# The last head pair's sample retention among its query projections, its norm in two parts, and attention's loads in memory of their own

## The chip, the cores and the metric

The kernel runs on one core of one Trainium2 chip. The metric is the device time of one execution in microseconds, as the median of several timed runs. A core has five engines that run their own instruction streams side by side and wait for each other by semaphores: TensorE (PE in the profile, its weight loads PEld), VectorE (DVE), ScalarE (ACT), GpSimd (POOL) and SyncE (SP, which issues most of the DMAs).

## The reference

One decoder layer over a prompt of 1024 tokens and 8 x 4 sample tokens. A combined projection of width 3912 feeds two groups of heads: sparse attention (8 heads, the top 256 keys chosen by an indexer) and retention (8 heads of 64, in chunks of 128 with a state carried from chunk to chunk). Each group's output is gated, both go through one output projection, a norm and a gated embedding. What the change touches is the retention, its head norm and gate, and the beginning of attention:

```python
def _head_norm(o):
    mu = jnp.mean(o, axis=-1, keepdims=True)
    var = jnp.mean(jnp.square(o - mu), axis=-1, keepdims=True)
    return (o - mu) * lax.rsqrt(var + EPS)
...
    def step(S, inp):
        qc, kc, vc = inp
        inter = jnp.einsum('bchk,bhkv->bchv', qc * dec_in[None, :, :, None], S)
        scores = jnp.einsum('bchk,bshk->bhcs', qc, kc) * dmat[None]
        intra = jnp.einsum('bhcs,bshv->bchv', scores, vc)
        S = S * dec_chunk[None, :, None, None] + jnp.einsum('bchk,bchv->bhkv', kc * dec_out[None, :, :, None], vc)
        return S, inter + intra
...
    logits = jnp.einsum('bqngd,bqknd->bqngk', qg, kg.astype(jnp.float32)) * (HEAD_DIM ** -0.5)
...
    logits = jnp.where(sel_ok[:, :, None, None, :], logits + bias, -jnp.inf)
    probs = jax.nn.softmax(logits, axis=-1)
    o = jnp.einsum('bqngk,bqknd->bqngd', probs, vg.astype(jnp.float32))
...
    yb = jax.nn.silu(gb) * _head_norm(ob).reshape(B, T, D_B).astype(x.dtype)
```

The retention runs once over the prompt (8 chunks of 128 tokens, state 0 at the start) and once over the samples (one chunk of 4 tokens for each of 8 requests, with a state that is read from memory and written back).

## The kernel before

The work goes in phases: the input norm and the indexer's scores, the sample's selection of keys, the retention, attention over the prompt with the sample's attention woven in, the output projection, and the gated embedding. A scheduler of the framework orders each engine's instructions; between them the order is by the sequence of the code, by priority, and by what is ready in its own reckoning. Semaphores are placed after that. An engine never passes over a waiting instruction.

The retention loops over four pairs of heads (hp 0 to 3). For a pair it makes, in this order: the sample's q and k (mm_s, 32 rows, L274, summed from four partial results by a copy on ACT, L276, and three adds on VectorE, L279); for each of eight blocks of 128 tokens (tb) a q/k projection into a PSUM bank named pqk (mm_a, 24 matmuls, L265 to L267), rotated by rope (three VectorE products L1034 to L1036 into tiles rp, one buffer each, then two additions on POOL, L1038 and L1039); then the rotation of the sample's q and k; the sample's v and gate (mm_s again); and for each block a v/g projection (bank pvg). ACT takes v and the gate out of that bank (L1047, L1049). Then the chunk's recurrence follows: transposes (L1055, L1056), a copy of qkT by ACT (L1060), scores (L1065), the decay mask by VectorE (sm, L1066), the state update (L1456, sbd L1461), two products (L1465, L1467) and a copy of the result into acc (L1469). pqk and pvg take turns in the same three PSUM banks.

At block 7 comes the sample's retention, ret_sample: its state s0 is loaded, qm (VectorE, L1113) and eight products L1116 (16 matmuls in the profile) apply it, L1118 adds the scores' part, L1120 and L1122 collect it in acc, vm (L1127) and dst (L1129) make the new state, sso (L1133, L1134), which is stored (L1135). qm, vm and sso share one memory (tag vm). Last comes norm_gate, over the eight prompt blocks and then over the sample's rows: statistics (L1075, L1076), a root on ACT with one refinement on VectorE (L1081 to L1090), the scaling on ACT and VectorE (L1094, L1096), the gate (L1099, for the last pair on VectorE) and the store into yb_d (L1100). acc has one buffer, so the next pair's results wait for that store.

steps(hp) weaves in the sample's selection (bits oh, L1246, matmuls psl, L1248, then le, row and idx, L1252 to L1260, which feed POOL's gathers L1147).

Attention goes over eight query blocks (qb) and two key heads (kv). For each it makes near (L1550, the position bias from toep), scores sa on TensorE (L1563, L1564, a bank of three), their masked sum and row minimum mn on VectorE (L1569), the exponential on ACT (L1572), transposes ptp and a copy pT, the product ob with the values vtok, and the reciprocal sums spread by rb. Its loads are qas (queries, two buffers), toep, vtok and the keys ka. The first weights of the output projection (o0) are loaded, cast (L179) and subtracted (L180) by load_w.

The sample's retention and the norm in the last pair stand here:

```python
            if tb == 7:
                sgS = ret_sample(hp, qks[8], sh, acc)
        steps(hp)
        ...
        norm_gate(acc, sgs, 8, 128, 0, hp)
        norm_gate(acc[:, 8:9, :], [sgS], 1, NS, 8, hp)
```

## Time and profile before

| what | value |
|---|---|
| median of 3 runs | 1076.51 us (1073.67 to 1078.84) |
| profiled execution | 1065.73 us, its span 1063.9 us |
| granted TensorE clock, mean | 0.973 |
| busy, share of the span | PE 93%, PEld 79%, DVE 66%, ACT 47%, POOL 27% |
| last v/g projection of the last pair | starts at 636.19 us |
| first attention scores | start at 651.86 us |

The profiled execution is one run with the profiler on; its time is 1% below the median of the timed ones. Times in its rows count from the start of the span. A row of the timeline has the start, the duration, the engine, the line, the operation, output and inputs by the program's names, partitions x elements and type, a count, and in brackets the idle time ahead of it with what ended it. A row of a window has its length and the busy time of each engine with the number of instructions, then the granted TensorE clock (1 is full), the DMA engines' mean share and GB/s.

### The profile page before, as it was taken

How to read it: one execution, taken by the hardware profiler on the slowest of the kernel's cores; microseconds unless marked ns; L12 is line 12 of the kernel's file. 1: busy time of each engine (PE TensorE's matmuls, PEld its weight loads, DVE VectorE, ACT ScalarE, POOL GpSimd, SP SyncE). 2: the span in 40 equal slices, each digit the busy share in tenths (PEclk: the TensorE clock that was granted, in tenths of full speed). 3: DMA queues.
4: the chain of work that ended last, by engine and by line, in shares of the span. 5: the costliest groups of instructions: out<-in, count | busy, mean ns of one | idle time of the engine just before them, and what ended most of it. 6: DMA issues, size and time to landing. Idle time of an engine off the chain costs nothing.

```text
span 1063.9 us, 19686 instructions
## 1 busy us (share of the span) xinstructions
PE 991.7 (93%) x7375; PEld 838.6 (79%) x7375; DVE 699.8 (66%) x2012; ACT 504.2 (47%) x1092; POOL 288.1 (27%) x287
## 2 busy tenths in 40 slices
...
GB/s 291 65 60 51 79 96 169 186 145 202 126 164 111 70 40 41 37 48 87 61 24 41 119 86 149 190 79 105 75 56 47 117 41 80 148 111 82 86 37 40
DMA packets 98308, 102.24 MB, mean 96 GB/s; under 512 B 21346, under 2 KB 88386, under 8 KB 95906
## 3 DMA queue, kind: packets, MB, share of 16 engines
...
## 4 chain that ended last, share of the span: by engine, by line
PE 53%; DVE 8%; ACT 2%; DMA 2%; issue 1%; POOL 1%; SPq 0%; DVEq 0%; ACTq 0%; POOLq 0%
PE ob L1587 4%; PE ptp L1579 4%; PE pg L265 3%; PE pg L267 3%; PE pg L266 3%; PE po L265 3%; PE po L266 2%; PE po L267 2%; PE pvg L265 2%; PE pvg L266 2%; PE pvg L267 2%; PE sa L1563 2%; PE sa L1564 2%; PE pqk L265 2%; PE pqk L266 1%; PE pqk L267 1%
## 5 line engine op out<-in xcount | busy, mean ns | idle before, releaser
L1147 POOL DMA_INDIRECT kvs<-in_cache_kv,idx x64 | 63.6, 994 | 84.1 <-ACT pT L1584 44.7
L265 PE MATMUL pqk<-whi_qkb,xh 128*128 128x256 f32 x256 | 74.5, 291 | 5.5 <-DVE rp L1036 5.5
L265 PE MATMUL pvg<-whi_vgb,xh 128*128 128x256 f32 x256 | 77.4, 302 | 1.6 <-DVE need L729 1.5
L266 PE MATMUL pvg<-wlo_vgb,xh 128*128 128x256 f32 x256 | 76.6, 299 | 0.0
L267 PE MATMUL pvg<-whi_vgb,xl 128*128 128x256 f32 x256 | 75.2, 294 | 0.0
L266 PE MATMUL pqk<-wlo_qkb,xh 128*128 128x256 f32 x256 | 73.5, 287 | 0.0
L265 PE MATMUL po<-whi_o,yTh 128*128 128x256 f32 x256 | 73.1, 286 | 0.4 <-DVE yaT L1598 0.4
L267 PE MATMUL pqk<-whi_qkb,xl 128*128 128x256 f32 x256 | 73.0, 285 | 0.0
L267 PE MATMUL po<-whi_o,yTl 128*128 128x256 f32 x256 | 72.8, 285 | 0.0
L265 PE MATMUL pg<-whi_g,yTh 128*128 128x256 f32 x256 | 72.7, 284 | 0.0
L266 PE MATMUL po<-wlo_o,yTh 128*128 128x256 f32 x256 | 72.7, 284 | 0.0
L267 PE MATMUL pg<-whi_g,yTl 128*128 128x256 f32 x256 | 72.3, 282 | 0.0
L266 PE MATMUL pg<-wlo_g,yTh 128*128 128x256 f32 x256 | 72.2, 282 | 0.0
L500 DVE SCALAR_TENSOR_TENSOR score<-r,wi,score 128x384 f32<-128x384 f32 (+5 forms) x42 | 44.2, 1053 | 21.0 <-ACT r L496 19.9
L1572 ACT ACTIVATE L<-L,mn 128x128 f32<-128x128 f32 (+7 forms) x64 | 49.5, 775 | 13.7 <-DVE mn L1569 13.6
L265 PEld LDWEIGHTS pqk<-whi_qkb,xh 128*128 128x128 f32 x256 | 48.2, 188 | 9.6 <-issue 6.8
L1768 DVE TENSOR_TENSOR sgm<-pu,sgm 128x256 f32<-128x256 f32 x32 | 13.5, 423 | 61.8 <-PE pu L267 58.6
L265 PEld LDWEIGHTS pvg<-whi_vgb,xh 128*128 128x128 f32 x256 | 50.6, 197 | 3.7 <-issue 1.7
L266 PEld LDWEIGHTS pvg<-wlo_vgb,xh 128*128 128x128 f32 x256 | 50.7, 198 | 0.5
L267 PEld LDWEIGHTS pvg<-whi_vgb,xl 128*128 128x128 f32 x256 | 50.6, 198 | 0.6
L265 PEld LDWEIGHTS po<-whi_o,yTh 128*128 128x128 f32 x256 | 49.0, 191 | 2.2 <-issue 1.6
L496 ACT ACTIVATE r<-si 128x384 f32<-128x384 f32 (+5 forms) x48 | 36.3, 758 | 30.3 <-PE si L354 29.0
...
## 6 DMA issues: line engine op xcount, KB each, us to landing
...
```

Source lines behind the costliest of these rows:

```text
L265: nc.tensor.matmul(pt[:, :n], ah, hi[:, k, :n], start=(k == 0), stop=False)
L266: nc.tensor.matmul(pt[:, :n], ah, lo[:, k, :n], start=False, stop=False)
L267: nc.tensor.matmul(pt[:, :n], al, hi[:, k, :n], start=False, stop=(k == kc - 1))
L496: nc.scalar.activation(r[:, :n], s[:, :n], AF.Relu)
L500: nc.vector.scalar_tensor_tensor(sc, r[:, :n], wi[:, qb, h:h + 1], sc, op0=ALU.mult, op1=ALU.add)
L1147: return nc.gpsimd.indirect_dma_start(out=dst, out_offset=None, in_=kvflat, in_offset=bass.IndirectOffsetOnAxis(ap=idx, axis=0))
L1563: nc.tensor.matmul(s[:, :wc], qas[:, h, :], kah[kv][:, c:c + wc], start=True, stop=False)
L1564: nc.tensor.matmul(s[:, :wc], qas[:, h, :], kal[kv][:, c:c + wc], start=False, stop=True)
L1572: behind[0] = nc.scalar.activation(L[:, :n], L[:, :n], AF.Exp, bias=least, scale=-1.0, accum_out=sm[:, i4:i4 + 1])
L1579: nc.tensor.transpose(tp[:, i4 * 128:i4 * 128 + 128], P[i4][:, kb * 128:kb * 128 + 128], ident)
L1587: nc.tensor.matmul(ob[64 * o:64 * o + 64, :256], vtok[:, kb, kv * 64:kv * 64 + 64], pT[:, o * 256:o * 256 + 256], start=(kb == 0), stop=(k ...
L1768: nc.vector.tensor_tensor(sg[:rows], usrc, sg[:rows], op=ALU.mult)
```

## The change

For the last pair (hp 3) the sample's q and k are rotated ahead of block 0; at block 4 of the q/k projections the sample's v and gate are projected and its retention is made; at block 4 of the v/g projections the sample's rows and blocks 0 to 3 are normed and gated; blocks 4 to 7 are normed at the end. The other pairs keep their order. Attention's queries, toep and vtok get a pool of their own on the other side of the memory, opened ahead of the keys' loads. One bank of the scores' phase is set aside first (lfirst), which turns the order in which the others are handed out. The first output weights' load is put behind the exponentials of the third query block.

```diff
--- before.py
+++ after.py
@@ -1433,16 +1433,22 @@
         sh = mm_s(bank("pqk"), xs, wqk, 256, rt, f"qk{hp}")
         wvg = load_w(f"vgb{hp}", wcols((VB + hp * 128, 128), (GB + hp * 128, 128)))
         qks = []
+        if hp == 3:
+            qk8 = rope(sh, NS, 8, f"{hp}_8")
         for tb in range(8):
+            if hp == 3 and tb == 4:
+                acc = rt.tile([128, 9, 128], F32, tag="acc", bufs=1, name=f"acc{hp}")
+                sh = mm_s(bank("pvg"), xs, wvg, 256, rt, f"vg{hp}")
+                sgS = ret_sample(hp, qk8, sh, acc)
             pt = bank("pqk")
             mm_a(pt, xlhs, wqk, 256, tb)
             qks.append(rope(pt, 128, tb, f"{hp}_{tb}"))
             steps(hp)
-        qks.append(rope(sh, NS, 8, f"{hp}_8"))
-        acc = rt.tile([128, 9, 128], F32, tag="acc", bufs=1, name=f"acc{hp}")
         sgs = []
-        sh = mm_s(bank("pvg"), xs, wvg, 256, rt, f"vg{hp}")
         if hp < 3:
+            qks.append(rope(sh, NS, 8, f"{hp}_8"))
+            acc = rt.tile([128, 9, 128], F32, tag="acc", bufs=1, name=f"acc{hp}")
+            sh = mm_s(bank("pvg"), xs, wvg, 256, rt, f"vg{hp}")
             wnext = load_w(f"qkb{hp + 1}", wcols((QB + (hp + 1) * 128, 128), (KB + (hp + 1) * 128, 128)))
         for tb in range(8):
             pt = bank("pvg")
@@ -1467,16 +1473,22 @@
                 nc.tensor.matmul(o[:, j * 64:j * 64 + 64], sm[:, j, :], vv[:, j * 64:j * 64 + 64],
                                  start=(tb == 0 and j == 0), stop=(j == 1))
             nc.scalar.copy(acc[:, tb, :], o)
-            if tb == 7:
+            if tb == 7 and hp < 3:
                 sgS = ret_sample(hp, qks[8], sh, acc)
+            if hp == 3 and tb == 4:
+                norm_gate(acc[:, 8:9, :], [sgS], 1, NS, 8, hp)
+                norm_gate(acc, sgs, 4, 128, 0, hp)
         steps(hp)
         so = rt.tile([128, 64], F32, tag="so", bufs=2, name=f"so{hp}")
         for j in range(2):
             js = slice(j * 64, j * 64 + 64)
             nc.vector.tensor_scalar(so[js], sbd[0][js, js], gend[js, hp:hp + 1], None, op0=ALU.mult)
         nc.sync.dma_start(O["ret_state_prompt"][0, 0, 2 * hp:2 * hp + 2].rearrange("h d v -> (h d) v"), so)
-        norm_gate(acc, sgs, 8, 128, 0, hp)
-        norm_gate(acc[:, 8:9, :], [sgS], 1, NS, 8, hp)
+        if hp < 3:
+            norm_gate(acc, sgs, 8, 128, 0, hp)
+            norm_gate(acc[:, 8:9, :], [sgS], 1, NS, 8, hp)
+        else:
+            norm_gate(acc[:, 4:8, :], sgs[4:], 4, 128, 4, hp)
     rt_stack.close()
     bss_.close()
 
@@ -1484,6 +1496,22 @@
         for _ in ss:
             pass
     ka = [wp.tile([128, 2, T], F32R, tag=f"w{t}", bufs=2, name=f"ka{t}") for t in ("hi", "lo")]
+    pres = ExitStack()
+    pre = pres.enter_context(pool("pre"))
+    vtok = pre.tile([128, 8, 128], F32, name="vtok")
+    toep = pre.tile([128, 8, 256], F32, name="toep")
+
+    def load_q(qb):
+        q = pre.tile([128, 8, 128], F32R, tag="qas", bufs=2, name=f"qas{qb}")
+        last_q[0] = nc.sync.dma_start(q.bitcast(F32), qas_d[:, :, qb * 128:(qb + 1) * 128]).ins
+        return q
+
+    last_q = [None]
+
+    qnext = load_q(0)
+    nc.sync.dma_start(toep, bass.AP(tensor=toep_d.tensor, offset=toep_d.offset + 127,
+                                    ap=[[8 * 384 - 1, 128], [384, 8], [1, 256]]))
+    nc.sync.dma_start(vtok, v_d)
     kah, kal = ([t[:, i] for i in range(2)] for t in ka)
     for i in range(2):
         for a, t in enumerate((kah[i], kal[i])):
@@ -1499,25 +1527,12 @@
     yaT = yap.tile([128, 4, T], F32, name="yaT")
     psum_phase(b=3, t=2, l=1, o=1)
     kept["tags"] = "s"
+    bank("lfirst", "l")
     as_ = ExitStack()
     ap_ = as_.enter_context(pool("att", side="right"))
     a1 = ExitStack()
     atl = a1.enter_context(pool("atl", side="right"))
     at = a1.enter_context(pool("at1", side="right"))
-    vtok = ap_.tile([128, 8, 128], F32, name="vtok")
-    toep = ap_.tile([128, 8, 256], F32, name="toep")
-
-    def load_q(qb):
-        q = ap_.tile([128, 8, 128], F32R, tag="qas", bufs=2, name=f"qas{qb}")
-        last_q[0] = nc.sync.dma_start(q.bitcast(F32), qas_d[:, :, qb * 128:(qb + 1) * 128]).ins
-        return q
-
-    last_q = [None]
-
-    qnext = load_q(0)
-    nc.sync.dma_start(toep, bass.AP(tensor=toep_d.tensor, offset=toep_d.offset + 127,
-                                    ap=[[8 * 384 - 1, 128], [384, 8], [1, 256]]))
-    nc.sync.dma_start(vtok, v_d)
     a2 = ExitStack()
     kp = a2.enter_context(pool("kp", side="right"))
     kvs.extend(kp.tile([128, 8, 256], F32, name=f"kvs{i}") for i in range(NKV, 4))
@@ -1571,6 +1586,8 @@
                             least, i = mn[:, i:i + 1], i + 1
                 behind[0] = nc.scalar.activation(L[:, :n], L[:, :n], AF.Exp, bias=least, scale=-1.0,
                                                  accum_out=sm[:, i4:i4 + 1])
+                if qb == 2:
+                    late = behind[0].ins
                 more(0.4 + n / 1200)
             ob = bank("ob", "o")
             for kb in range(qb + 1):
@@ -1606,6 +1623,7 @@
     a1.close()
     as_.close()
     s3.close()
+    pres.close()
     s1.close()
     lps.close()
 
@@ -1642,7 +1660,8 @@
             return tiles[tb][0][:, k, :], tiles[tb][1][:, k, :]
         return f
 
-    wt = [load_w("o0", [(w_out[:, 0:256], 256)])]
+    with tc.issue_after(late):
+        wt = [load_w("o0", [(w_out[:, 0:256], 256)])]
     for tb in range(8):
         yb = mg.tile([128, 512], F32, tag="yb", bufs=3, name="yb")
         nc.sync.dma_start(yb, yb_d[:, tb].rearrange("p a b -> p (a b)"))
```

In the built program this moves instructions as follows; a name's last number tells tiles apart. The first place is VectorE at the end of pair 2 and the start of pair 3's q/k projections: sbd0 is pair 2's state, rp13_0 the rotation of block 0 of pair 3, rp13_8 that of its sample rows, oh and le the selection. Before:

```order
L1461 TENSOR_TENSOR sbd0_3313<-ret_6727,sbd1_3314 64x64 x2
L1034 TENSOR_TENSOR rp13_0_7029<-pqk_7004,cst_63 128x256
L1035 TENSOR_TENSOR rp23_0_7030<-pqk_7004,cst_63 128x4x32
L1036 TENSOR_TENSOR rp23_0_7030<-pqk_7004,cst_63 128x4x32
L1066 TENSOR_TENSOR sm_6779<-ret_6774,cst_63 128x128
L1066 TENSOR_TENSOR sm_6779<-second_3327,cst_63 128x128
L1246 TENSOR_SCALAR oh_5348<-slot16_5082,sm6_5077 128x256
L1246 TENSOR_SCALAR oh_5352<-slot16_5082,sm6_5077 128x256
```

and now:

```order
L1467 TENSOR_TENSOR sbd0_3313<-ret_6727,sbd1_3314 64x64 x2
L1066 TENSOR_TENSOR sm_6779<-ret_6774,cst_63 128x128
L1066 TENSOR_TENSOR sm_6779<-second_3327,cst_63 128x128
L1246 TENSOR_SCALAR oh_5348<-slot16_5082,sm6_5077 128x256
L1246 TENSOR_SCALAR oh_5352<-slot16_5082,sm6_5077 128x256
...
L1034 TENSOR_TENSOR rp13_8_7004<-sh_qk3_6987,cst_63 32x256
L1035 TENSOR_TENSOR rp23_8_7005<-sh_qk3_6987,cst_63 32x4x32
L1036 TENSOR_TENSOR rp23_8_7005<-sh_qk3_6987,cst_63 32x4x32
...
L1034 TENSOR_TENSOR rp13_0_7037<-pqk_7012,cst_63 128x256
L1035 TENSOR_TENSOR rp23_0_7038<-pqk_7012,cst_63 128x4x32
L1036 TENSOR_TENSOR rp23_0_7038<-pqk_7012,cst_63 128x4x32
```

The rotation of block 0 stood right behind the state sum; it now stands 58 rows further on, behind the sample's rotation, which waits for three adds L279.

The second place is TensorE's end of the last pair, around the second products of the last block. Before, the sample's matmuls stand between the block's products and the first scores sa:

```order
L1465 MATMUL ret_7649<-sbd1_3314,qkT_7652 128x128
L1467 MATMUL ret_7649<-vv3_7_7644,sm_7654 128x64 x2
L1116 MATMUL ret_7673<-s0_3315,qm_7683 32x128 x8
L1118 MATMUL ret_7673<-vvs3_7668,sm_7678 32x64 x2
L1129 MATMUL dst_7699<-vm_7700,qk3_8_7270 64x512
L1129 MATMUL dst_7699<-vm_7703,qk3_8_7270 64x512
L1563 MATMUL sa_7862<-kahi_7808,qas0_7842 128x128
L1564 MATMUL sa_7862<-kalo_7809,qas0_7842 128x128
```

and now, where ret_7710 is block 6 and ret_7757 block 7 (L1471 and L1473 are the old L1465 and L1467, L1578 the old L1563):

```order
L1471 MATMUL ret_7710<-sbd0_3313,qkT_7713 128x128
L1473 MATMUL ret_7710<-vv3_6_7705,sm_7715 128x64 x2
L1462 MATMUL ret_7757<-vv3_7_7752,qk3_7_7330 128x128
L1471 MATMUL ret_7757<-sbd1_3314,qkT_7760 128x128
L1473 MATMUL ret_7757<-vv3_7_7752,sm_7762 128x64 x2
L1578 MATMUL sa_7880<-kahi_7822,qas0_7829 128x128
L1579 MATMUL sa_7880<-kalo_7823,qas0_7829 128x128
L1578 MATMUL sa_7887<-kahi_7822,qas0_7829 128x128
```

The sample's matmuls L1116 to L1129 have left; the scores follow block 7 directly.

The third place is ACT between the last copy into acc and the first exponentials (L1572, now L1587). Before, all twelve scalings of the norm and those of the sample's rows stand ahead of the first exponential:

```order
L1084 ACTIVATE gy_7750<-gv_7749 128x16
L1094 ACTIVATE acc3_7276<-acc3_7276,gz_7751,gy_7750 128x64 x12
L1084 ACTIVATE gy_7792<-gv_7791 32x2
L1094 ACTIVATE acc3_7276<-acc3_7276,gz_7793,gy_7792 32x64 x2
L1572 ACT_TABLE_LOAD
L1572 ACTIVATE L_7860,sm_7859<-L_7860,mn_7861 128x128
L1572 ACTIVATE L_7867,sm_7859<-L_7867,mn_7868 128x128
L1572 ACTIVATE L_7875,sm_7859<-L_7875,mn_7876 128x128
```

and now:

```order
L1475 COPY acc3_7144<-ret_7757 128x128
L1587 ACT_TABLE_LOAD
L1587 ACTIVATE L_7878,sm_7877<-L_7878,mn_7879 128x128
L1587 ACTIVATE L_7885,sm_7877<-L_7885,mn_7886 128x128
L1587 ACTIVATE L_7893,sm_7877<-L_7893,mn_7894 128x128
L1084 ACT_TABLE_LOAD
L1084 ACTIVATE gy_7797<-gv_7796 128x8
L1587 ACT_TABLE_LOAD
L1587 ACTIVATE L_7900,sm_7877<-L_7900,mn_7901 128x128
```

Three exponentials come first, then a root of the second half's norm (L1084) between two table loads; that half's scalings L1094 come later, among the exponentials of the second query block.

## The prediction, made before the changed kernel ran

> **What bounds the kernel now.** I read the page first, then the busy times by window around the last pair, then TensorE's waits there, then the timelines of the engines it waits for.
>
> The windows (columns: stretch; its length; busy us of PE, PEld, DVE, ACT, POOL with their instruction counts; granted clock; DMA share; GB/s):
>
> ```profile
> PE 991.7 (93%) x7375; PEld 838.6 (79%) x7375; DVE 699.8 (66%) x2012; ACT 504.2 (47%) x1092; POOL 288.1 (27%) x287
> ...
> 576.00:606.00 30.00, 30.00 (x281) 26.46 (x281) 29.47 (x123) 8.37 (x22) 11.74 (x23) 1.00 0.24 59
> 616.00:636.00 20.00, 20.00 (x171) 18.99 (x170) 9.47 (x51) 5.08 (x21) 2.52 (x4) 1.00 0.12 34
> 640.00:650.00 10.00, 6.71 (x46) 3.63 (x44) 8.51 (x33) 3.46 (x10) 3.09 (x2) 0.70 0.87 261
> 655.00:660.00 5.00, 0.00 (x0) 0.00 (x0) 3.35 (x15) 3.82 (x13) 0.00 (x0) 0.50 0.24 67
> 670.00:700.00 30.00, 30.00 (x220) 19.45 (x219) 26.53 (x104) 19.94 (x57) 16.65 (x18) 0.98 0.50 148
> ```
>
> TensorE is the bound: 93% of the span, and 100% of it on both sides of one hole. The hole lies between the last pair's last projection and the point at which attention runs without gaps. Inside it the clock falls to 0.50. A second fact matters as much: in the last pair's q/k projections (576 to 606) VectorE is full too, 29.47 of 30, and in the value and gate projections after them (616 to 636) it is half idle, 9.47 of 20.
>
> The hole on TensorE, first its waits from 636 to 666 (total, times, longest), then its rows (start, duration, idle time before and its releaser):
>
> ```profile
> PE sa L1563 <- DVE mn L1569: 7.9, 1, 7.9
> ...
> 636.19 0.28 PE L267 MATMUL pvg<-whi_vgb,xl 128*128 128x256 f32 x1
> 639.48 0.56 PE L1467 MATMUL ret<-vv,sm 128*128 128x64 f32 x4
> 643.88 0.79 PE L1465 MATMUL ret<-sbd,qkT 128*128 128x128 f32 x2 [1.93 <-DVE sbd L1461]
> 645.35 1.08 PE L1116 MATMUL ret<-s,qm 128*32 128x128 f32 x16
> 649.97 1.96 PE L1129 MATMUL dst<-vm,qk 32*64 32x512 f32 x2 [0.77 <-DVE vm L1127]
> 651.86 0.47 PE L1563 MATMUL sa<-kahi,qas 128*128 128x128 f32 x1
> 661.29 0.48 PE L1563 MATMUL sa<-kahi,qas 128*128 128x128 f32 x1 [7.89 <-DVE mn L1569]
> 665.57 1.13 PE L1594 MATMUL rb<-cst,rs 128*64 128x128 f32 x8
> ```
>
> The last projection starts at 636.19, the first attention score at 651.86 (15.7 us later), and the first row of sums to be spread (rb) at 665.57. From there to 700 PE is full. So the stretch to be judged is 665.57 - 636.19 = 29.4 us. What fills it on the other two engines:
>
> ```profile
> 641.68 1.69 DVE L1113 TENSOR_TENSOR qm<-qkT,cst 128x256 f32<-128x256 f32 x1
> 654.24 0.98 DVE L1096 TENSOR_SCALAR acc<-acc,bmv,gy 128x64 f32<-128x64 f32 x4
> 660.94 0.29 DVE L1569 CUSTOM_DVE_ANT_0 L<-sa,near 128x128 f32<-128x128 f32 x1
> ...
> 637.27 1.98 ACT L179 CAST whi_o<-wraw_o 128x1024 fp32r<-128x1024 f32 x2
> 639.63 0.36 ACT L1060 COPY qkT<-ret 128x256 f32<-128x256 f32 x1
> 647.13 1.28 ACT L1084 ACT_TABLE_LOAD   x1
> 648.43 0.22 ACT L1084 ACTIVATE gy<-gv 128x16 f32<-128x16 f32 x1
> 654.36 4.09 ACT L1094 ACTIVATE acc<-acc,gz,gy 128x64 f32<-128x64 f32 x12 [5.71 <-DVE gz L1090]
> 661.31 1.28 ACT L1572 ACT_TABLE_LOAD   x1 [0.72 <-DVE mn L1569]
> ```
>
> Two things are in series: the sample rows' retention (qm to the second dst), and the norm of all eight blocks, in front of attention's first row minimum (L1569) in VectorE's order.
>
> **Term 1, the hole.** In the new order nothing of the sample is left behind the last projection, and the first L1584 (old L1569) stands right behind the statistics of block 7. I walk the new order with the durations above. In the old run block 6's chain ended with the products at 639.48, 640.0 or 3.8 after 636.19. Block 7's copy of qkT then waited for the two casts (637.27 to 639.25) and its state sum for qm (1.69); both are gone from there. Transposed scores, mask, state sum and two products of block 7 are about 2.5 us, so the first score comes 6.0 to 6.5 after the last projection. VectorE reaches the first minimum some 0.5 later, after the statistics of block 7, near 7.0. From the first minimum to rb took 665.57 - 660.94 = 4.6. In the new ACT order a square root, with a table load each way, stands between the third and the fourth exponential: 2 x 1.28 + 0.22 = 2.8 in the chain. That makes 6.5 + 0.5 + 4.6 + 2.8 = 14.4 where 29.4 stood: **-15.0 us**. I keep half clock in it, as it was there before; bounds -17 (the square root hides behind scores) and -12 (the chain of block 7 is as slow as before).
>
> The Trainium skill ("ScalarE: Activation LUTs", "What ACT_TABLE_LOAD costs") gives about 1.28 us for a load plus about 1.38 of drain. The load agrees with 1.28 here; but the root began at 648.43, 0.02 after the load of 647.13 was over, and no drain shows. By the page the two loads would add 2.8 more, and term 1 would be about -12.
>
> **Term 2, the price amid the q/k projections.** The sample's retention moves to where VectorE has nothing to spare. Worse than its own work is what its place does to the order. The rotation of the sample's q and k is now VectorE's first rotation, and it needs the complete sample projection; rotation 0 stood behind pair 2's state sum before and now stands behind three partial adds, four rounds of the selection and pair 2's sample work. Projections share three memory banks, so each projection waits for the rotation three banks back: blocks 3 to 7 of q/k and blocks 0 to 2 of v/g hang on it. What the new order has ahead of rotation 7 that the old had behind it costs, by the mean of each row (VectorE by line, 570 to 606):
>
> ```profile
> L1246 DVE TENSOR_SCALAR oh<-slot,sm 128x256 bf16<-128x256 bf16 x24 | 8.3, 395 | 0.5 <-PE psl L1248 0.5
> L1252 DVE TENSOR_TENSOR le<-psl,cst 128x384 bf16<-128x384 f32 x7 | 3.8, 545 | 0.0
> L1257 DVE TENSOR_REDUCE row<-le 128x6 f32<-128x384 bf16 x7 | 3.7, 534 | 0.0
> L1133 DVE TENSOR_TENSOR sso<-dst,s 64x512 f32<-64x512 f32 x2 | 1.4, 684 | 0.0
> L1127 DVE TENSOR_TENSOR vm<-vvs,cst 32x512 f32<-32x512 f32 x2 | 1.3, 672 | 0.0
> L279 DVE TENSOR_TENSOR sh_qk<-pqk,sh_qk 32x256 f32<-32x256 f32 x3 | 1.3, 419 | 0.1
> ...
> 603.52 0.41 DVE L1034 TENSOR_TENSOR rp<-pqk,cst 128x256 f32<-128x256 f32 x1
> 603.85 0.27 DVE L1035 TENSOR_TENSOR rp<-pqk,cst 128x128 f32<-128x128 f32 x1
> ...
> 601.30 0.36 PE L265 MATMUL pvg<-whi_vgb,xh 128*128 128x256 f32 x1
> 609.00 0.36 PE L265 MATMUL pvg<-whi_vgb,xh 128*128 128x256 f32 x1
> ...
> 584.53 0.63 PE L1116 MATMUL ret<-s,qm 128*32 128x128 f32 x12
> L1129 PE MATMUL dst<-vm,qk 32*64 32x512 f32 x4 | 2.1, 612 | 0.0
> ```
>
> 8 x 0.395 + 3 x 0.545 + 3 x 0.534 + 2 x 0.684 + 2 x 0.672 + 3 x 0.419 = 10.4; a rotation of the sample, 1.0; some twenty small ones at 0.15 to 0.4, 3.0: 14.4 in all. Neighbours start before the one ahead ends (603.52 + 0.41 is 603.93, and the next began at 603.85), about 0.075 for each of 45: 3.4 less, so 11.0. Rotation 7 then ends not at 604.3 but near 615.3. The third v/g block (24 matmuls each from 601.30, so it began at 609.00) waits for it: 6.3 late, if VectorE never idles. It will idle a little, since its chain with TensorE has become tighter. I add 1 and take 7.3. Of this TensorE spends 3 on the sample's own matmuls (16 of L1116 about 1.0, the dst pair 1.1, scores and products 0.9), and about 0.7 on selection matmuls that it then need not do later. So the last v/g projection is 7.3 - 0.7 = **+6.6 us** late; VectorE's half-idle 616 to 636 comes too late to win that back, since TensorE is full there. Bounds: +3 (only the sample's matmuls, all else hidden) and +13 (14.4 without overlap, 9.7 late, and 3 or so of idling).
>
> **Term 3, attention's start.** The second half of the norm (four L1096-like or gate operations and small ones, about 3 us of VectorE; six L1094 at 4.09 / 12, 2 us of ACT), and the output weights' casts (2 x 1.98) and their subtraction on POOL, now lie in 660 to 700. There VectorE has 3.5 of 30 free and ACT 10; TensorE is full and owes what they cannot cover. I take **+2.0**; bounds 0 (all in free time) and +6.
>
> New waits come with the move. On VectorE the sample's qm shares its memory with pair 2's new state, and stands until that has been stored (L1135); rotation 3 and all later rotations are queued behind it. About 4 us of other work lie between the state and qm in the order, which should cover a store. On TensorE the sample's second products (L1118, amid q/k block 7) need a copy that ACT makes behind twelve L1094, 4.09; the rest of block 7 is queued behind them. Both are the 1 us of idling above, and its 3 at the bound. The sample's two state loads, its store and POOL's two additions for the rotation move along; POOL has 11.74 busy of 30 there, and SP's queue sets the store ahead of attention's keys.
>
> The loads in memory of their own are costed at nothing: their cover is the v/g projections (616 to 636 with a DMA share of 0.12), and if it were gone the first score would wait for the queries behind the other loads, at most the 10 us from 640 to 650 in which they hold a DMA share of 0.87. The bank set aside lets the scores use banks that no late chain holds; its gain is already in the 6.5.
>
> **Sum.** -15.0 + 6.6 + 2.0 = -6.4 us on the profiled execution's 1065.73, so 1059.3. The three timed runs have a median of 1076.51, 1% above it; I carry the ratio over: 1076.51 x 1059.3 / 1065.73 = 1070.0.
>
> **The rivals.** First, the pass gives it back: term 2 is at +12, since every wait of TensorE on VectorE is followed by one of VectorE on TensorE. For it speaks 29.47 of 30; against it that VectorE's idle time there is so small (0.5 ahead of all L1246) that TensorE's answers must have been ready. -15.0 + 12 + 2 = -1, so 1075.5: no change.
>
> Second, slower: the clock. After a hole of 3.87 us TensorE ran at half rate for some 6 us of full work, and even 1.93 was enough at 643.88, where two L1465 took the same 0.79:
>
> ```profile
> 545.73 0.79 PE L1465 MATMUL ret<-sbd,qkT 128*128 128x128 f32 x2 [3.87 <-DVE sbd L1461]
> ...
> 546.00:548.00 2.00, 2.00 (x10) 2.00 (x11) 1.68 (x13) 0.25 (x1) 0.00 (x0) 0.50 0.00 0
> 552.00:554.00 2.00, 2.00 (x20) 2.00 (x20) 1.93 (x9) 0.29 (x2) 0.00 (x0) 1.00 0.00 0
> ```
>
> If the waits of the q/k pass reach 2 us, each spell costs 3 us of work, and a block, 3.85 with what lies between (two from 601.30 to 609.00), takes nearly twice that, longer than VectorE's round (a rotation every 30 / 7 = 4.3 us from 576 to 606): the two wait for each other in turn. Term 2 at its upper end and two such spells, 13 + 6, give -15.0 + 19 + 2 = +6, so 1082.5. It decides from a delay of 13 us on the third v/g block. The Trainium skill ("TensorE: Matmul & The Clock Gate", "What's actually happening") says the clock halves after an idle window of about 3.4 us that runs freely. By that rule gaps of 2 us would mostly be harmless and this rival nearly void; the row at 643.88 went down after 1.93, though behind a stretch that had smaller gaps, so I keep it.
>
> Third, the change doesn't do what it says: ACT reaches the copy of the sample's rows into acc (L1120, now between v/g blocks 0 and 1), which may overwrite pair 2's rows only once their store has landed. That store waited until 619.2 for POOL's gathers:
>
> ```profile
> 619.20 0.43 ACT L1469 COPY acc<-ret 128x128 f32<-128x128 f32 x2 [3.89 <-DMA yb_d<-acc]
> ```
>
> Behind L1120 stand the value copies of block 1, which release the bank of v/g block 4. With the pass 7 late they are due near 622, so 619 to 622 is hidden; if the gathers slip by as much again, some 6 us are lost: -6.4 + 6 = -0.4, 1076.1.
>
> **Chances.** Forecast 0.42. Its better end, with term 2 at its lower bound and term 3 at nothing, -15.0 + 3 + 0 = -12 or 1064.4: 0.16. First rival 0.15, second 0.20, third 0.07. What this kernel can tell from no change is about 0.5%, 5.4 us: of the forecast's own spread (-10 to -3, 1066 to 1073.5) I count 0.29 beyond it and 0.13 within. Faster is then 0.29 + 0.16 = 0.45; within 0.5% 0.13 + 0.15 + 0.06 = 0.34; slower 0.20 + 0.01 = 0.21. The range, 1062 to 1082, takes in the better end with a little for the spread of three runs (1073.67 to 1078.84), and reaches at the top nearly to the second rival.
>
> **What would show it.** Right: no sample line (L1116, L1129) behind the last v/g projection; first score 6 to 7 us after it, rb 14 to 15 after it; rotation 7 near 615 and TensorE waits with releaser rp L1036 or L279 of 6 us in all between 578 and 615; clock 1.00 there; a table load, a square root and another load between exponentials. Wrong: waits over 2 us with clock 0.50 before 616 (second rival), an ACT wait on yb_d at L1120 beyond 622 (third), scores waiting for a DMA, or TensorE gaps after rb.

## The result: slower by about one per cent

The changed kernel took 1091.04 us (median of six runs, 1085.68 to 1095.35) beside 1077.22 of the kernel before: a ratio of 1.0133, 95% interval 1.0111 to 1.0155. Timed again later, with before beside it (experiment e17), the ratio was 1.0079, 1.0051 to 1.0106. The change is slower both times, and its size is somewhere from 0.8% to 1.3%. The forecast was 1070.0 us, faster, from a median of 1076.51 for before; with that median the two ratios give 1091 and 1085, both above the forecast's range of 1062 to 1082.

The profiled execution of the change took 1094.28 us, span 1092.5. That of before (1065.73) lay 1% below its own median, so I do not compare the two spans. I compare one stretch: from the last pair's first q/k projection (566.6 before, 568.7 in the change) to attention's output projection (825.5 and 849.1). The windows of before over its three parts, the q/k and v/g pass, the hole and the first 60 us of attention (length; busy us of PE, PEld, DVE, ACT, POOL; clock; DMA share; GB/s):

```profile
566.60:636.20 69.60, 69.60 (x613) 63.10 (x612) 54.46 (x231) 24.27 (x70) 25.37 (x37) 1.00 0.32 85
636.20:665.60 29.40, 17.33 (x97) 11.36 (x95) 19.81 (x85) 16.11 (x46) 6.20 (x4) 0.63 0.48 139
665.60:725.60 60.00, 60.00 (x439) 39.23 (x440) 49.28 (x189) 37.85 (x101) 31.88 (x33) 0.95 0.47 139
```

The same parts in the change:

```profile
568.70:654.00 85.30, 76.92 (x643) 67.73 (x642) 62.15 (x260) 33.78 (x89) 24.96 (x37) 0.94 0.37 103
654.00:667.70 13.70, 8.92 (x63) 7.18 (x61) 10.37 (x52) 9.17 (x27) 1.64 (x1) 0.84 0.41 112
667.70:727.70 60.00, 46.03 (x302) 29.63 (x302) 37.06 (x151) 31.52 (x86) 31.15 (x28) 0.84 0.37 108
```

The hole shrank by 15.7 us. The pass ahead of it grew by 15.7: TensorE, without a gap before, now stands 8.4 us in it, and 76.92 - 69.60 = 7.3 more go to busy time. In the first 60 us of attention, where TensorE had no gap, it now stands for 14.0 us. The three traces of the change differ in that last part, and the stretch sums up as follows (rb is the first spread of the row sums, po the first output projection):

| trace | pass | hole | rb to po | stretch | against before |
|---|---|---|---|---|---|
| before | 69.6 | 29.4 | 159.9 | 258.9 | |
| change, first trace | 85.3 | 13.8 | 181.3 | 280.4 | +21.5 |
| change, second (e8) | 83.8 | 13.8 | 168.5 | 266.1 | +7.2 |
| change, third (e17) | 84.5 | 13.7 | 170.0 | 268.2 | +9.3 |

The first trace holds a stall of VectorE that the others lack. VectorE's rows there (the bracket gives the idle time and what ended it), and the window over it with no matmul at all:

```profile
696.43 0.08 DVE L1584 DVE_READ_ACCUMULATOR2_ANT mn<- 128x1 f32 x1
705.20 0.42 DVE L1614 TENSOR_TENSOR gat<-rb,gat 128x256 f32<-128x256 f32 x1 [8.69 <-remote]
...
697.00:702.00 5.00, 0.00 (x0) 0.00 (x0) 0.00 (x0) 0.00 (x0) 3.78 (x5) 0.55 0.37 105
```

The view names no releaser (`remote`); the last section says what L1614 waited for. I take a stretch of +7 to +9 for the change; in the trace with the stall attention is 11 to 13 us longer than in the other two.

The steps that the prediction named are to be seen in TensorE's rows after the last projection in the change:

```profile
653.96 0.28 PE L267 MATMUL pvg<-whi_vgb,xl 128*128 128x256 f32 x1
656.56 0.49 PE L1462 MATMUL ret<-vv,qk 128*128 128x128 f32 x2 [0.42 <-DVE sm L1066]
659.33 0.49 PE L1471 MATMUL ret<-sbd,qkT 128*128 128x128 f32 x2 [0.57 <-DVE sbd L1467]
660.02 0.31 PE L1578 MATMUL sa<-kahi,qas 128*128 128x128 f32 x1
...
667.73 1.13 PE L1611 MATMUL rb<-cst,rs 128*64 128x128 f32 x8
```

No matmul of the sample's retention (L1116 to L1129) is left there, the first score comes 6.1 us after the last projection, and rb 13.8 after it. In the pass, TensorE's longest waits of the change (total, times, longest):

```profile
PE pqk L265 <- DVE sh_vg L279: 2.3, 1, 2.3
PE ret L1462 <- DVE sm L1066: 1.5, 1, 1.5
PE ret L1471 <- DVE sbd L1467: 1.3, 2, 1.0
PE pqk L265 <- DVE rp L1036: 1.0, 2, 0.6
PE pvg L274 <- DVE rp L1036: 1.0, 1, 1.0
...
```

They are small and many, all with VectorE as releaser, and two of them have a spell of half clock beside them. The windows from the wait of 1.0 at 581.8 and from the wait of 2.3 that ended at 608.8:

```profile
581.80:588.30 6.50, 6.47 (x47) 5.77 (x48) 6.37 (x28) 0.52 (x2) 0.00 (x0) 0.50 0.04 8
588.30:608.70 20.40, 15.65 (x149) 12.24 (x147) 18.91 (x73) 6.22 (x17) 9.64 (x18) 1.00 0.35 98
608.70:612.00 3.30, 3.24 (x15) 3.27 (x16) 3.30 (x11) 3.25 (x5) 2.12 (x5) 0.51 0.00 0
```

Half of 6.47 + 3.24 is 4.9 us lost to the clock. So the pass's 15.7 is 8.4 of standing, 4.9 of half clock, and some 2.4 that are left for the sample's own matmuls (3 by the prediction, less 0.7). In the second and third trace it is 5.7 and 6.2 of standing, 6.8 for 13.7 us at half clock, and 1.7 to 1.8 that are left.

### The profile page after: what moved, and what is told of

Same layout as the page of the kernel before. It is cut to its first block, busy times and chain, and to the rows that moved or that the text cites. A ratio compares the mean times of both kernels' runs of the same rounds, so it can differ in the third digit from the quotient of the medians.

```text
span 1092.5 us, 19673 instructions
## 1 busy us (share of the span) xinstructions
PE 1000.8 (92%) x7375; PEld 848.0 (78%) x7375; DVE 701.2 (64%) x2019; ACT 512.3 (47%) x1098; POOL 287.4 (26%) x287
## 4 chain that ended last, share of the span: by engine, by line
PE 65%; DVE 18%; ACT 6%; DMA 4%; issue 3%; SPq 1%; another core or an unknown queue 1%; POOL 1%; DVEq 0%; ACTq 0%; POOLq 0%
PE pb L255 4%; PE pb L256 4%; PE pb L257 4%; PE ptp L1596 4%; PE ob L1604 4%; PE po L265 3%; PE po L266 2%; PE po L267 2%; PE pg L265 2%; PE pg L267 2%; PE pg L266 2%; PE pox L811 2%; PE sa L1578 2%; ACT js L655 2%; PE pqk L265 2%
## 5 line engine op out<-in xcount | busy, mean ns | idle before, releaser
L267 PE MATMUL pg<-whi_g,yTl 128*128 128x256 f32 x256 | 72.9, 285 | 0.0
L1587 ACT ACTIVATE L<-L,mn 128x128 f32<-128x128 f32 (+7 forms) x64 | 49.5, 777 | 25.7 <-DVE mn L1584 22.2
L1596 PE MATMUL ptp<-cst,L 128*128 128x128 f32 x288 | 48.9, 291 | 13.4 <-DVE gat L1614 10.0
L1596 PEld LDWEIGHTS ptp<-cst,L 128*128 128x128 f32 x288 | 32.1, 144 | 37.0 <-issue 20.5
L265 PEld LDWEIGHTS pqk<-whi_qkb,xh 128*128 128x128 f32 x256 | 50.5, 197 | 12.8 <-issue 5.6
L1786 ACT ACTIVATE sgm<-pg 128x256 f32<-128x256 f32 x32 | 12.3, 385 | 84.0 <-PE pg L267 71.0
L267 PEld LDWEIGHTS pqk<-whi_qkb,xl 128*128 128x128 f32 x256 | 50.5, 197 | 1.3 <-issue 1.0
```

Of the source, the lines that this page charges most:

```text
L265: nc.tensor.matmul(pt[:, :n], ah, hi[:, k, :n], start=(k == 0), stop=False)
L267: nc.tensor.matmul(pt[:, :n], al, hi[:, k, :n], start=False, stop=(k == kc - 1))
L1587: behind[0] = nc.scalar.activation(L[:, :n], L[:, :n], AF.Exp, bias=least, scale=-1.0, accum_out=sm[:, i4:i4 + 1])
L1596: nc.tensor.transpose(tp[:, i4 * 128:i4 * 128 + 128], P[i4][:, kb * 128:kb * 128 + 128], ident)
```

## The experiments

All ratios are to the kernel before, run on the same chip beside the experiment, with the 95% interval. "Stretch" is as above. There is one trace of each kernel, three of the change. The stretch less that of before is within 3.7 us of the difference of the timed medians in every experiment but e8, so I read its parts as parts of the time, to no better than that. e8 is one execution, of 1085.02 beside a median of 1070.94: 14.1 more, of which the stretch holds 7.2. Most of the rest lies ahead of the stretch, which began at 574.75 there, 8.1 later than in before; in the other traces that point lies between 565.1 and 575.4.

| kernel | ratio | pass | hole | rb to po | stretch |
|---|---|---|---|---|---|
| before | 1 | 69.6 | 29.4 | 159.9 | 258.9 |
| e1 change without own memory | 1.0093 (1.0067 to 1.0119) | 83.9 | 20.3 | 164.8 | 269.0 |
| e2 change, gathered-row tiles reversed | 1.0060 (1.0028 to 1.0091) | 83.4 | 13.7 | 166.4 | 263.5 |
| e3 only the sample's retention and norm moved | 1.0107 (1.0051 to 1.0163) | 84.7 | 20.1 | 163.6 | 268.4 |
| e4 retention in the v/g pass, norm in two parts | 1.0020 (0.9997 to 1.0043) | 72.5 | 26.5 | 160.9 | 260.0 |
| e5 e4 with own memory, tiles reversed | 0.9982 (0.9960 to 1.0004) | 72.7 | 20.6 | 166.1 | 259.3 |
| e6 change, rotation written later | 1.0066 (1.0040 to 1.0092) | 73.5 | 17.1 | 174.8 | 265.5 |
| e7 own memory, bank, late weights alone | 0.9998 (0.9975 to 1.0022) | 69.6 | 22.5 | 166.7 | 258.9 |
| e9 e6, kvs1 in the loads' memory | 1.0046 (1.0024 to 1.0068) | 72.9 | 28.3 | 163.4 | 264.6 |
| e10 e4 with own memory, kvs1 in it | 1.0116 (1.0090 to 1.0141) | 72.5 | 32.3 | 169.7 | 274.6 |
| e11 change, kvs1 in the loads' memory | 1.0147 (1.0113 to 1.0181) | 84.9 | 25.6 | 163.6 | 274.1 |
| e12 change, kvs1 at the front | 1.0088 (1.0053 to 1.0123) | 83.2 | 12.9 | 170.3 | 266.5 |
| e13 e6, kvs1 at the front | 1.0004 (0.9981 to 1.0026) | 72.5 | 16.7 | 168.8 | 258.0 |
| e14 e7, kvs1 at the front | 1.0011 (0.9994 to 1.0029) | 69.7 | 21.5 | 168.7 | 259.9 |
| e15 change without the second root | 1.0060 (1.0035 to 1.0086) | 84.3 | 11.2 | 169.4 | 264.9 |
| e16 e13 without the second root | 0.9978 (0.9957 to 0.9998) | 72.7 | 13.7 | 168.8 | 255.3 |
| e17 the change again | 1.0079 (1.0051 to 1.0106) | 84.5 | 13.7 | 170.0 | 268.2 |

**What the pass costs, and why: e3, e4, e6.** e3 takes before and moves only the sample's retention among the q/k projections, its early rotation included, with the norm of its rows in the v/g pass:

```diff
+        if hp == 3:
+            qk8 = rope(sh, NS, 8, f"{hp}_8")
         for tb in range(8):
+            if hp == 3 and tb == 4:
...
+                sgS = ret_sample(hp, qk8, sh, acc)
             pt = bank("pqk")
...
+            if hp == 3 and tb == 4:
+                norm_gate(acc[:, 8:9, :], [sgS], 1, NS, 8, hp)
```

> The kernel before with the sample's retention amid the q/k projections (and the norm of the sample's rows at block 4 of v/g); the prompt's norm is whole and at the end, no own memory, no bank set aside, output weights loaded as before. Theory A: the q/k and v/g passes end about 15 us late, as in the changed kernel; the stretch from the last v/g projection to the first rb falls from 29.4 to about 21; attention takes its 160 again; so about +6 us, 1083. Rival: the 15 us come from the norm's first half in the v/g pass; then the passes end at most 8 late and the time is 1076 or less.

It loses 1.07% by itself, with a pass of 84.7. So the loss of the change is there without its memory, bank or late weights. e4 moves the retention to the v/g pass instead, and splits the norm:

```diff
-            if tb == 7:
+            if tb == (3 if hp == 3 else 7):
                 sgS = ret_sample(hp, qks[8], sh, acc)
```

> The kernel before with the sample's retention at block 3 of the v/g pass, where VectorE is half idle, and the norm in two parts as in the change; no own memory, no bank set aside, output weights as before. Theory A: the last v/g projection is late by little more than the sample's matmuls, 3 to 5 us; from it to the first rb 15 to 20 us instead of 29.4; attention 160 to 164; time about 1070, faster by 0.5 to 1%. Rival: ACT with its extra table loads becomes the limit of the v/g pass, the passes end over 8 us late, and the time is 1077 or more.

There the same work costs the pass 2.9 us, not 15. The forecast for the rest missed: the first score still came 15.2 us after the last projection, where it was 15.7, the hole was 26.5, and the time did not change beyond its interval (1.0020). e6 is the change with two lines moved, so that the retention stays amid the q/k projections and only the rotation of the sample's rows is written later:

```diff
-        if hp == 3:
-            qk8 = rope(sh, NS, 8, f"{hp}_8")
         for tb in range(8):
+            if hp == 3 and tb == 4:
+                qk8 = rope(sh, NS, 8, f"{hp}_8")
             if hp == 3 and tb == 4:
```

> As the change, but the rotation of the sample's q and k is written just ahead of the sample's retention at q/k block 4 instead of ahead of block 0. VectorE's order then has rotations 0 to 3 ahead of it again. If the early rotation's place in VectorE's order is what makes the pass longer (each projection waits for the rotation three banks back), the stretch from the first q/k projection to the last value and gate projection takes 75 to 79 us rather than 85.3, and the ratio to before is 1.003 to 1.007. If it is the sample's own work and its chain of waits between TensorE and VectorE, wherever the rotation stands, the stretch stays at 83 to 86 and the ratio at 1.010 to 1.014.

The pass fell to 73.5. VectorE's rotations tell why. Times of the change are from its first trace. In the change the sample's rotation (rp<-sh_qk) is first, and rotation 0 follows it at 592.44, 23.8 us after the first projection; the last begins at 621.27:

```profile
587.75 0.40 DVE L1034 TENSOR_TENSOR rp<-sh_qk,cst 32x256 f32<-32x256 f32 x1
592.44 0.42 DVE L1034 TENSOR_TENSOR rp<-pqk,cst 128x256 f32<-128x256 f32 x1
...
621.27 0.43 DVE L1034 TENSOR_TENSOR rp<-pqk,cst 128x256 f32<-128x256 f32 x1
```

In e6 rotation 0 begins at 568.85, 3.8 us after the first projection, as before (570.38, also 3.8 after), the sample's stands behind rotation 3, and the last begins at 605.11. Its window over the pass has TensorE busy for all but 1.1 us and the clock at 1.00:

```profile
568.85 0.42 DVE L1034 TENSOR_TENSOR rp<-pqk,cst 128x256 f32<-128x256 f32 x1 [0.54 <-PE pqk L267]
588.09 0.38 DVE L1034 TENSOR_TENSOR rp<-sh_qk,cst 32x256 f32<-32x256 f32 x1
...
605.11 0.41 DVE L1034 TENSOR_TENSOR rp<-pqk,cst 128x256 f32<-128x256 f32 x1
565.10:638.60 73.50, 72.44 (x624) 63.14 (x623) 59.64 (x238) 27.19 (x73) 24.94 (x37) 1.00 0.44 120
```

TensorE's rows show where the change loses this time. Its only waits for a rotation in the pass, and the start of the third v/g block:

```profile
593.31 0.39 PE L265 MATMUL pqk<-whi_qkb,xh 128*128 128x256 f32 x1 [0.46 <-DVE rp L1036]
...
597.72 1.07 PE L274 MATMUL pvg<-wraw_vgb,xs 128*32 128x256 f32 x16 [0.99 <-DVE rp L1036]
599.34 0.39 PE L265 MATMUL pqk<-whi_qkb,xh 128*128 128x256 f32 x1 [0.55 <-DVE rp L1036]
...
626.07 0.36 PE L265 MATMUL pvg<-whi_vgb,xh 128*128 128x256 f32 x1
```

Counted from the pair's first projection, the third q/k block starts 16.3 us in, where it started at 8.1; the fourth 24.6 (12.9), the fifth 30.7 (16.5), the first v/g block 49.1 (34.7), the third 57.4 (42.4). So nearly all is lost by the fifth q/k block, 14.2 late. The order of TensorE itself is another there: pair 2's sample products (L1116 at 583.30) stand ahead of the third block at 584.99, and stood behind the start of the fifth before (584.53, 583.10). In e6 the third block starts at 573.19, ahead of them (583.87) again.

That settles the pass: the sample's work costs 3.9 there, and the place of one rotation, with the order that comes of it, 10 to 12. The timed gain was smaller than the pass's, because e6 took 174.8 in attention; e13 comes back to that.

**What the loads' own memory does: e1, e2, e7, e8.** e1 is the change with vtok, toep and the queries back in attention's pool:

```diff
-    pre = pres.enter_context(pool("pre"))
-    vtok = pre.tile([128, 8, 128], F32, name="vtok")
...
+    vtok = ap_.tile([128, 8, 128], F32, name="vtok")
```

> The changed kernel, but attention's queries, toep and vtok are back in attention's own pool, loaded where they were loaded before; all other parts stay. Theory A (the loss in attention is the memory: with the loads in a pool of their own the sample's gathered rows move onto the last pair's acc, so the first gather waits for the store of the norm's second half, 681.9 in the changed kernel against 665.0 before): the first gather comes back to within 5 us of rb's start, the stretch from the first rb to the first output projection falls from 181 to about 163, and the time from 1091 to about 1076. Theory B (the loss in attention is the second half of the norm itself, its two table loads and the late casts, all still here): the stretch stays above 175 and the time above 1086.

The first gather came back to 0.6 us ahead of rb, as theory A had it. The hole is 6.5 longer and attention 3.7 to 5.2 shorter than in the second and third trace of the change. The ratio, 1.0093, lies between the two of the change (1.0079 and 1.0133), so no difference in time can be told. What I had noticed is that the own memory moves other tiles: the gathered rows of the sample (kvs1 to kvs3) come to lie on the last pair's acc, which is still to be stored. The last gate of the norm's second half, its store and POOL's first gather in the change's first trace:

```profile
675.66 0.69 DVE L1099 TENSOR_TENSOR acc<-acc,sg 128x128 f32<-128x128 f32 x3
...
676.37 0.37 SPq L1100 DMA_DIRECT2D yb_d<-acc  x1
...
681.94 0.95 POOL L1147 DMA_INDIRECT kvs<-in_cache_kv,idx  x1 [3.44 <-PE sa L1579]
```

The norm's second half is made amid attention's first scores and ends 8.6 us behind rb (676.35); its store leaves at once, and the gathers come after the store, 14.2 us behind rb. Before, the first came at 665.02, 0.6 ahead of rb. e2 lays the three tiles out in reverse:

```diff
-    kvs.extend(kp.tile(..., name=f"kvs{i}") for i in range(NKV, 4))
+    kvs.extend([kp.tile(..., name=f"kvs{i}") for i in range(3, NKV - 1, -1)][::-1])
```

> The changed kernel with one edit: the three tiles of gathered rows are laid out in reverse order, so that the first one used no longer lies on acc but on small tiles of the norm, which are free about 8 us earlier and need no store. Theory A: the first gather starts near 674 instead of 682 on the changed kernel's clock, the stretch from rb to the output projection falls by 6 to 10 from 181, time about 1083. Theory B: no change, 1091.

The first gather came 11.8 us behind rb, not the 6 or so of theory A. Attention was 166.4 against 168.5 and 170.0, and the ratio 1.0060 beside 1.0079 and 1.0133, each with its interval: at most a small gain. e7 is before with the own memory, the bank set aside and the late output weights alone (retention and norm as before):

> Before, with the loads in memory of their own, the bank set aside and the late output weights, but the sample's retention and the whole norm at the end of the pair, as before. Theory (the gathered-row tiles come to lie on the last pair's outputs, so that POOL's second gather waits until the norm's outputs are stored): the pass stays at 69 to 71 us, the first gather comes 5 to 12 us after the spread sums instead of 0.6 ahead of them, attention takes 163 to 170 instead of 159.9, and the ratio is 1.002 to 1.009. Rival (memory of their own costs nothing): attention 160 to 162, the hole of 29.4 us shorter by 1 to 3, ratio 0.997 to 1.000.

A hole of 22.5 instead of 29.4 and an attention of 166.7 instead of 159.9: the sum is 189.2 against 189.3, and the time the same. Neither theory had it: the own memory gains 7 us, and attention takes them back. e8 is the change itself, for one more trace:

> The change itself once more, for its trace. In its first trace VectorE stood 8.7 us at 696.5 with no releaser that the trace shows, and attention took 181.4 us. If this belongs to the change, a gap of 7 to 10 us without a shown releaser comes again on VectorE within 30 us of the first gathers, and attention takes 178 to 184. If it was chance of that one execution, the gap is gone and attention takes 170 to 174 (166.4 of the reversed layout and 3 to 4 more for gathers 4 us later, and what else the later second gather costs).

The stall of VectorE was gone, attention took 168.5, and the stall is not in the third trace either. The first theory of this run falls: it does not belong to the change in each execution.

**Are the held-back gathers what lengthens attention? e9 to e14.** e5 put the better places together: retention in the v/g pass, norm in two parts, own memory, tiles reversed.

> The sample's retention stands behind the fourth block of the value and gate projections, where VectorE is half idle, instead of amid the q/k projections; the norm in two parts, the loads' own memory, the bank set aside and the late output weights stay as in the change, and the gathered-row tiles are laid out in reverse, so that none lies on the last pair's outputs that are still being stored. Theory (the place amid the q/k projections costs 14 to 15 us, the place of the gathered rows the rest): the stretch from the first q/k projection of the last pair to its last value and gate projection takes 72 to 74 us (69.6 before, 85.3 in the change), the first score 6 to 7 after it, the spread sums 7 to 8 after that, attention from there to its output projection 161 to 165; sum against before +3 - 15.5 + 2 to +5 = -7 to -10, so a ratio of 0.990 to 0.994. Rival (memory of their own costs attention as such, wherever the tiles lie, since it was still 6.5 longer in the reversed layout): attention 166 to 168, ratio 0.996 to 1.000.

It is the fastest kernel with the whole computation, but 0.9982 with an interval that takes in 1 is no gain that can be told; attention took 166.1, as the rival had it. e9, e10 and e11 put kvs1 into the loads' own memory, so that the first gathers don't wait for the last pair:

```diff
     toep = pre.tile([128, 8, 256], F32, name="toep")
+    kvs.append(pre.tile([128, 8, 256], F32, name="kvs1"))
```

> As the kernel with the later rotation (e6), and the tile of the first gathered rows (kvs1) lies beside the queries, the Toeplitz block and the values in their own memory, so that POOL's first gathers wait for nothing of the last pair, neither outputs nor stores. Theory (attention's length is set by the later of two chains, TensorE's own from the spread sums and the sample's from POOL's first gather, 152 to 163 us from first gather to the sample's last product in every run so far; the change hurries the first and holds the second back): first gather within 4 us of the spread sums, attention 160 to 165 instead of 174.9, pass 73 to 74, hole 16 to 18, ratio to before 0.991 to 0.996. Rival (attention takes longer by itself when it begins amid the last pair's norm, whenever the gathers start): attention 170 to 175, ratio 1.000 to 1.006.

> The sample's retention behind the fourth block of the value and gate projections (as in e5), the gathered-row tiles in their usual order, but kvs1 in the memory of the loads. Theory: as e5 but with the first gather earlier: pass 72.6, hole 20 to 21, attention 161 to 164 instead of 166.1, so 254 to 258 from the pair's first projection to attention's output projection against 258.9 before, ratio 0.994 to 0.998. Rival (the gathers were no limit in e5): attention stays at 165 to 167, ratio 0.998 to 1.001.

> The change, with nothing else different than that kvs1 lies in the memory of the loads, so that the first gathers don't wait for the store of the last norm. Theory (of the change's loss, the pass holds about 14 and the held-back gathers the rest): pass 83 to 85, hole 13 to 14, first gather at the spread sums (within 3 us instead of 14 to 15 behind), attention 160 to 164, so 257 to 262 from first projection to output projection against 258.9 before: ratio 0.998 to 1.003. Rival (the gathers' place is harmless, and attention is slower for the norm and the casts that moved into it): attention 166 to 170, ratio 1.006 to 1.010.

All three miss, and mix two things: the first gather did come at rb (0.3 us ahead of it), but with these 8 KB more per partition the queries' loads came late: in e11 the first was issued at 670.74, behind the last store, and in the change at 633.81, ahead of the last projection. (Which tiles the queries came to lie on no view shows.) The first score came 17.4 to 24.3 us after the last projection (TensorE's longest wait for qas was 3.6 to 4.0). What they give is the price of late loads: in e11 the hole is 25.6 instead of 13.8. Their traces also have TensorE's signals late (last section), so their parts are less sure than the others. e12, e13 and e14 put kvs1 at the front of attention's memory instead, where the last projections' inputs lay, and leave the loads early:

```diff
+    kvs.append(ap_.tile([128, 8, 256], F32, name="kvs1"))
     a1 = ExitStack()
```

> The change, with only the tile of the first gathered rows (kvs1) moved to the front of attention's memory, where the inputs of the last projections lay, so that the first gathers wait neither for the last norm's outputs nor for a store, and the queries' loads stay as early as in the change (in e9 to e11 they had become late). Theory: pass 83 to 85, hole 13 to 14, first gather no later than the spread sums, attention 160 to 164: 257 to 262 from the pair's first projection to attention's output projection against 258.9 before, ratio 0.998 to 1.004. Rival (the place of the gathers is harmless; attention is longer for the norm half and the casts that lie in it now): attention 166 to 170, ratio 1.006 to 1.012.

> As e12 and the sample's rotation written just ahead of its retention (as in e6). Theory: pass 73 to 74, hole 16 to 18, attention 160 to 165, together 250 to 256 against 258.9, ratio 0.990 to 0.996. Rival (attention cannot begin ten us earlier and keep its length, since its sample half is paced by something other than the gathers' memory): attention 170 to 175, ratio 1.002 to 1.007.

> As e7 (own memory, bank set aside and late output weights alone; retention and norm as before), with kvs1 at the front of attention's memory. Theory: pass 69.6, hole 22 to 23, attention 160 to 164, together 252 to 256 against 258.9, ratio 0.992 to 0.997. Rival (as in e7, attention gives back what the hole gains): attention 166 to 168, ratio 0.998 to 1.002.

In e12 the first gather came 0.2 us ahead of rb (rb at 662.45):

```profile
662.26 0.94 POOL L1147 DMA_INDIRECT kvs<-in_cache_kv,idx  x1 [2.46 <-ACT L L1588]
```

Yet attention took 170.3, as in the change, and the ratio 1.0088 is the change's. My theory that the gathers' place lengthens it falls for the change, and for e14 beside e7. In e13 it may hold: it takes 6.0 off e6's attention, by one trace each, and comes to 1.0004, between its two expectations. TensorE's waits of e12 from rb to po, and the first 60 us of its attention:

```profile
PE ppt L1352 <- DVE pr L1348: 3.1, 1, 3.1
PE ptp L1597 <- ACT L L1588: 3.0, 1, 3.0
PE sa L1579 <- DVE mn L1585: 1.8, 2, 1.4
PE pkg L1324 <- DMA kvs<-in_cache_kv,idx: 1.3, 2, 0.8
...
662.50:722.50 60.00, 53.73 (x381) 35.70 (x381) 49.77 (x180) 37.34 (x99) 32.79 (x29) 0.91 0.41 120
```

Against before (60.00 busy at 0.95) there are 6.3 us of gaps, and the granted clock of 0.91 takes 0.04 x 60 = 2.4 more. They are waits for all of VectorE, ACT and the gathers in turn. In the second and third trace of the change TensorE stood 7.5 and 8.0 us from rb to po, 3.7 and 4.2 of them for the gathered rows; in e12 it stood 6.3, 1.3 of them for these rows. Before it stood 0.4. Free one wait, and the others stand in its place.

**One of these waits by itself: e15 and e16.** The root in the norm's second half, between attention's first exponentials, is left out: the variance is copied in its place, so blocks 4 to 7 of the last pair are scaled by something else than their root.

```diff
-        nc.scalar.activation(y_, v_, AF.Sqrt)
+        if hp == 3 and tb0 == 4:
+            nc.scalar.copy(y_, v_)
+        else:
+            nc.scalar.activation(y_, v_, AF.Sqrt)
```

> The change with the square root of the norm's second half left out (the variance is copied instead, so rows 4 to 7 of the last pair are scaled wrongly): ACT needs no table load amid attention's first exponentials. Theory (the root with a load each way costs about 3 us in attention's first chain, as the prediction's first term has it): first score to spread sums about 5 instead of 7.7, pass and the rest as in the change, ratio lower than the change's by 0.002 to 0.004 (1.009 to 1.012). Rival (the chain finds the time again in the attention that follows): ratio as the change's, 1.012 to 1.016.

> e13 with the square root of the norm's second half left out in the same way. Theory: first score to spread sums 4 to 5 instead of 6.9, TensorE's wait of 2.5 on the exponential gone, ratio to before 0.996 to 0.999. Rival (attention gives it back): spread sums earlier, attention as much longer, 0.999 to 1.003.

From the first score to rb it took 5.2 instead of 7.7, and 4.5 instead of 6.9. Attention did not take it back (169.4 and 168.8), and the ratios are lower than those of e17 and e13 by 0.0019 and 0.0026, 2 to 3 us each. By the traces the detour for the root costs its 2.4 to 2.5 us in full; the times agree, but their intervals overlap. (The range given for e15 was laid from 1.0133, and missed.)

**The change once more: e17.**

> The change itself, timed in more rounds, with a third trace. Its first trace took 21.5 us more than before from the last pair's first q/k projection to attention's output projection, of which 8.7 were a stall of VectorE with no releaser shown; its second trace took 7.2 more; every other kernel here was timed within 3 us of what that stretch showed. If the stall is common in the change, the ratio is 1.011 to 1.016 again, between the two traces, and times spread over 8 to 12 us. If it was rare, the ratio is 1.006 to 1.010.

1.0079, with times from 1078.87 to 1081.81 and no stall in its trace: by its own condition, the stall was rare there. The first timing was higher and its times spread over 10 us. One of its six executions was traced, has the stall and took 1094.28; whether the others had it is open.

## Why the prediction was wrong

The sum was -15.0 + 6.6 + 2.0 = -6.4 on the profiled execution. Measured on the same stretch, by the second and third trace: -15.6 + 14.2 to 14.9 + 8.6 to 10.1 = +7 to +9. Two steps failed: how VectorE's delay in the q/k pass reaches TensorE, and that attention would stay full.

**Term 1, the hole, was right.** Predicted 14.4 instead of 29.4; measured 13.7 to 13.8. The first score came 6.1 after the last projection (6.0 to 6.5 predicted). One condition did not hold: the granted clock in the hole was 0.84, not the half that I had kept. The root stood between the exponentials as said, at 2.8 by rows of before and 2.4 to 2.5 by e15 and e16:

```profile
663.11 1.28 ACT L1084 ACT_TABLE_LOAD   x1
664.40 0.21 ACT L1084 ACTIVATE gy<-gv 128x8 f32<-128x8 f32 x1
664.63 1.28 ACT L1587 ACT_TABLE_LOAD   x1
```

The root began 0.01 after the load's 1.28 was over. By the Trainium skill ("ScalarE: Activation LUTs", "What ACT_TABLE_LOAD costs") a drain of about 1.38 would be added for each load; none shows here either.

**Term 2 had the right mechanism and the wrong size: +6.6 predicted, +14 to +16 measured, above its upper bound of 13.** The step that failed is the one that turned VectorE's delay into TensorE's. I counted 11.0 us of work ahead of rotation 7, let 4.7 of them pass unseen, since the third v/g block came that much after rotation 7 (609.00 after 604.3), and added 1 for idling. Rotation 7 began at 621.27, or 52.6 after the pass's first projection, where it was 603.52 - 566.63 = 36.9 before: 15.7 later, not 11. VectorE was busy for 46.0 us of these 52.6 and for 33.0 of 36.9, so 13.0 of the 15.7 are work and 2.7 are waiting (1.18 of it for the state's products ahead of vm at 590.58). And the 4.7 were not free: no TensorE wait for a rotation comes after 599.34, the loss is there by the fifth q/k block, and the third v/g block was 15.0 late, not 7.3. I looked for the wait at the end of VectorE's queue, and it was at its beginning, in the first rounds of the three banks. TensorE stands 8.4 us of the pass in small waits, and the clock falls beside two of them. The second rival had that loop and priced it at 19, with spells that begin from waits of 2 us; one came with a wait of 1.00. With e6 the cheaper remedy is shown as well: the place of one rotation, which I had named as worse than the sample's own work and had not separated in the sum. The sample's own work is 3.9.

**The pause and the clock.** After the wait of 1.00 us that ended at 581.83 two L1471 took 0.80 us, where they took 0.49 at 578.14, and a projection's matmul later 0.41 until 588.12 and 0.28 after. I had kept the second rival against the Trainium skill ("TensorE: Matmul & The Clock Gate", "What's actually happening"), by whose idle window of about 3.4 us such gaps would be harmless. The trace of the change does not agree with that figure: a wait of 1.00 us had a spell of half clock beside it, after gaps of 0.27 and 0.66 within the four us ahead of it. The same wait has one in the second and third trace too (it ended at 587.91 and 581.42, and half clock ran from 587.7 and 583.1). The length of one wait does not decide it: the 1.53 us ahead of 630.33 left the clock at 1.00.

**Term 3 was wrong: +2.0 predicted with a bound of +6, measured +8.6 to +10.1.** The failing step is "VectorE has 3.5 of 30 free and ACT 10": I charged only the work that I saw moved into attention's start, and took TensorE's full 30 us there as given. What the runs show in its place: from rb to po TensorE stood 0.4 us before, and 7.5 and 8.0 in the second and third trace, and had 5.6 us at half clock before, 7.5 and 11.9 there. Every kernel that shortened the hole below 23 us had an attention of 163.6 to 174.8 instead of 159.9; most lie at 166 to 170. That this includes e7 and e14, in which neither retention nor norm moves, shows that it isn't the moved norm half alone. My reading is that attention was full before because the hole had been long: while TensorE stood in it, loads, casts and position biases ran ahead. That is argued, not shown. The length of the hole alone doesn't set it: e1 and e3, without memory of their own for the loads, had holes of 20 and an attention of 164.8 and 163.6; e7 had 22.5 and 166.7; and e10, whose loads came late, had 32.3 and 169.7. Of the hole's 15.6 us some 5.5 to 7 are left after attention (e8, e17). Which of the waits stands for how much stays open; only the root is settled, 2.4 to 2.5 us, and it counts in term 1.

**"The loads in memory of their own are costed at nothing"** came out as nothing in the time (e7: 0.9998, e14: 1.0011), but not for the reason given. The cover I named held (no score waited for a load), and they gained 7 us in the hole that attention took back. What I missed is that memory of their own moves other tiles: the first gather came 14.3 us behind rb in e7, and 0.6 ahead of it before. That this place is what attention gives back the 7 us for, e14 does not bear out.

**The rivals.** The first (the pass gives it back) came nearest with its +12 for the pass, and missed attention's +8.6 to +10. The second saw its signs come true: over 13 us on the third v/g block (15.0), and a wait over 2 us (2.27 at 608.76) with half clock before 616. Its 1082.5 also lies nearest to the measured time, but that is luck in part, by a sum in which the pass was 4 to 5 too large and attention 7 to 8 too small. The third did not decide: ACT reached L1120 at 628.15, later than the 622 I named, but behind "issue", not a store, and TensorE had only 1.5 us of gaps from 612 to 654.
